# A third seven-product job, GLA factors in both directions at once, and transposes' banks freed by ScalarE

## The chip, the cores and the metric

One core of a Trainium2 chip runs one launch of the kernel. The metric is the device time of a launch in microseconds; times shown beside each other are of runs on the same chip. TensorE multiplies, VectorE, ScalarE and GpSimd (POOL) work element by element, and SyncE (SP) issues the DMAs in the order in which they are written.

## The reference

A layer of a hybrid backbone for 1024 latent tokens (width 1024) and 256 context tokens, in float32:

```python
p = modulate(rms_norm(x), sh, sc) @ w_in      # one projection, 9248 columns, also for the context
# columns: gq gk gv gg lr | dq dk dv dg | m_gla m_diff
# GLA: 4 heads, chunks of 64, both directions, decays from lr; the latent scans start from the context's state
scores = (q * exp(cum - ref)) @ (k * exp(ref - cum)).T ; o = tril(scores) @ v + (q * exp(cum)) @ state
state  = exp(last) * state + (k * exp(last - cum)).T @ v
# differential attention: 8 heads, queries 1024, keys 256 + 1024
a = softmax(s1) - lam * softmax(s2) ; o_diff = a @ v
y = sigmoid(m_gla) * (A @ w_br_gla) + sigmoid(m_diff) * (B @ w_br_diff)   # A, B: normed, SiLU-gated branches
out = x + g * (y @ w_out)
```

## The kernel before

The program is written by generators that run under a `Driver` (lines 57 to 185): a planner in plain Python that keeps a modelled time for each engine and resumes whichever generator is due, by priority. What it decides is only the order in which instructions stand in each engine's queue; on the chip they run in that order, each as soon as the semaphores allow. Its costs are in `Engine` (a fixed part and a part for each element) and `LAT` (the time until another engine sees a result). Every operation is issued through helpers, so the trace shows nearly all matmuls on L335, transposes on L361, all other engines' work on L197 and all DMAs on L300; tiles tell them apart.

Each matrix product in three matmuls (`mm3`): both operands are split into a high and a low part, by a copy of ScalarE and a subtraction of VectorE, and hi*hi, hi*lo and lo*hi are summed in PSUM. Tiles have a tag with a fixed number of buffers (`TAGS`); `acq` waits until one is free, `rel` gives it back. A buffer of PSUM (tags `mm`, `tp`, `gs`, `go`, `gt`, `mb`, `b1`, `mc`, ...) is one bank.

The stages, in order of time:

1. Normalisation, then jobs for gk, gq and half of gg, the decays (`job_la`), and sums of the normed input's quarters (`sums`), which go to DRAM.
2. `pairs` (L986): gv and then dv, each of 1024 columns, in seven products of half size (Winograd's form of Strassen's scheme) in place of eight. `pair_weights` (L917) makes the sums of weight quarters, 28 splits a job. Each product runs over 5 token tiles (4 latent, one of context), 4 k and 3 matmuls: 7 x 5 x 12 = 420 matmuls of 512 columns a job. TensorE's banks are `mm`, `gs`, `go` (A), `tp`, `gt` (B).
3. The late stage: `stream` runs dk0, gg1, dk1, dg0, dq0, MG0, dq1, dg1 (each 512 columns over 8 or 10 token tiles, 24 matmuls a tile). MG0 is the first half of the GLA branch's merge gate m_gla: 4 slices of 128 columns by 2 halves of the tokens, 8 half tiles of 24 matmuls; ScalarE takes the tanh and the result goes to `d_m`. Between them, with higher priority, stand the four GLA heads (`gla_head`, L1350). A head loads its keys and decays, sums the decays along each of 10 chunks of 128 and each direction (`prep`: 20 scans of 128 columns, with a `yield` after each), makes the state keys (`kstates`, tile `ge`), the inter-chunk queries (`gqe`) and for each pair of chunks and direction the factors `gqr` and `gkk` (in `intra`: subtractions of VectorE into `gd` and `gx`, exponents of ScalarE, products), then scores `gsc`, the states `gsb` and `gsf` and the output (`forward`, `post`, tile `gp`). Heads 1 and 3 lie in `hk`, the memory of the normed context, which is free (tag `hc`) when the second tile of dk1 has been projected. `job_gate` computes the residual gate's row `gb` on VectorE, from eight loads of `w_ada` into the tag `raw`, beside gg1.
4. When the stream has ended and GLA has (`to_gla`, `ev_b2`), the pools change and attention starts. `ev_b2` also lets the loads of queries (`aq`) and values (`vv`) go. 64 units (8 heads, 8 query tiles): scores for both softmaxes (`s`), maxima on VectorE, exponents `e` on ScalarE, the mix on VectorE, 10 transposes into banks of `b1` (`att_tr`), the split of the transposed weights (`split2`: of 10 blocks 8 by ScalarE's copy `ac` and GpSimd, the last 2 by ScalarE and VectorE from PSUM, tile `at`), products with the values (`att_av`) and for each two units the finish (`att_fin`, tile `b1k`) into `d_bT`.
5. Beside attention, at the lowest priority, `fill` (L1954) computes half tiles of 24 matmuls in the bank `mb`: the other 12 slices of the merge gates (kind 0), the 8 slices of A @ w_br_gla (kind 1), 40 half tiles that need no attention output, and then B @ w_br_diff (kind 2, 16 half tiles). The i-th may not start before unit `int(i * PACE)`. After the last scores the attention banks become `mc`, and the rest of the filler goes there; kind 2 needs `d_bT`.
6. The last projection, by seven products, with `gb` multiplied into w_out.

```python
            for c in (1, 0, 9, 8, 7, 6, 5, 4, 3, 2):                      # prep
                yield self.dve.tensor_tensor_scan(lab[:, c, 1:], self.ones, lab[:, c, 1:], 0.0, ALU.mult, ALU.add)
...
            e = self.act.activation(hi, pt, AF.Copy)                      # split2, pool is None
            yield On(e, "DVE")
            e = self.dve.tensor_tensor(lo, pt, hi.bitcast(F32), ALU.subtract)
            self.rel(tag, e)
```

## Time and profile before

| | |
|---|---|
| time, 3 runs | 1696.41, 1696.53, 1698.63 us |
| the profiled execution | 1694.84 us, span 1693.0 us, granted clock 0.995 |
| busy share of the span | PE 97%, weight loads 81%, DVE 70%, ACT 45%, POOL 36% |
| DMA | 292 MB, 173 GB/s on average |
| start of the seven-product jobs, late stage, attention | 208.26, 398.66, 912.35 us |
| last scores, start of the last projection's steady stretch | 1463.9, 1541.3 us |

A line of instructions has the line of the kernel, the engine, the operation, output<-input, the shapes and the count; behind the bar its busy time and the mean of one in ns; then the idle time just before it and what ended it. `128x512 f32` is 128 partitions of 512 columns.

### The profile page before, as it was taken

The page shows a single profiled execution, that of the slowest core. Times are in us where ns is not written, and L with a number is a line of the kernel's source. Part 1 is how long each engine was busy: PE and PEld are TensorE (multiplying, and loading weights), DVE is VectorE, ACT ScalarE, POOL GpSimd, SP SyncE. Part 2 cuts the span into 40 slices and gives each one's busy share as a digit, 9 for nine tenths or more (in the row PEclk, how much of TensorE's full clock was granted, in tenths as well). Part 3 has the DMA queues.
Part 4 walks back from the last instruction along what each step waited for, and adds up shares of the span by engine and source line. Part 5 has one row for each costly group of instructions (what it writes and reads, how often), then busy time and mean ns, then how long its engine had stood idle before and what let it go on. Part 6 is the DMA issues. An engine that isn't in the chain of part 4 may idle for free.

```text
span 1693.0 us, 24682 instructions
## 1 busy us (share of the span) xinstructions
PE 1647.7 (97%) x8437; PEld 1365.5 (81%) x8437; DVE 1179.3 (70%) x2179; ACT 766.4 (45%) x1564; POOL 603.4 (36%) x725
## 2 busy tenths in 40 slices
PE   8999999999999999999998999999999999999999
PEld 3788888888888888888886887888888778887887
DVE  4786853456877978875763888687777687735794
ACT  4666532243334245344342656556556455521231
POOL 1600200002554455543551554555545545620000
PEclk9999999999999999999999999999999999999999
DMA  8564847568457545644456244345267653269421
GB/s 304 169 217 177 329 158 271 182 245 304 131 171 246 165 144 157 189 149 138 125 152 180 72 131 128 116 124 141 80 172 240 177 155 101 75 197 360 159 100 75
DMA packets 255053, 292.38 MB, mean 173 GB/s; under 512 B 21928, under 2 KB 177488, under 8 KB 254928
## 3 DMA queue, kind: packets, MB, share of 16 engines
q1 hardware_dynamic: 254928, 290.80, 53.8%
q8 instruction: 67, 1.10, 0.3%
q14 instruction: 58, 0.48, 0.1%
HBM read 193.74 MB, written 96.99 MB: 172 GB/s over the span
## 4 chain that ended last, share of the span: by engine, by line
PE 87%; DMA 5%; DVE 3%; ACT 2%; POOL 1%; issue 1%; SPq 1%; ACTq 0%; DVEq 0%
PE mm L335 34%; PE mb L335 10%; PE mc L335 9%; PE s L335 8%; PE b L335 5%; PE go L335 4%; PE b L361 4%; PE tp L335 3%; PE gs L335 3%; PE gt L335 3%; PE tp L361 2%; DVE sm L197 1%; DMA w<-in_w_ada 1%; DMA h<-d_bT 1%; PE mz L335 1%
## 5 line engine op out<-in xcount | busy, mean ns | idle before, releaser
L335 PE MATMUL mm<-w,h 128*128 128x512 f32 x1608 | 405.9, 401 | 0.8 <-DVE w L197 0.8
L335 PEld LDWEIGHTS mm<-w,h 128*128 128x128 f32 x1608 | 296.8, 188 | 61.9 <-DVE w L197 2.0
L197 DVE TENSOR_REDUCE sm<-s 128x1 f32<-128x1024 f32 (+1 forms) x192 | 196.2, 1040 | 58.2 <-PE s L335 49.1
L335 PE MATMUL mb<-h,wt 128*128 128x512 f32 x816 | 221.1, 405 | 5.2 <-DVE ft L197 2.7
L335 PE MATMUL s<-hk,aq 128*128 128x512 f32 (+1 forms) x768 | 180.4, 368 | 11.0 <-ACT e L197 9.4
L197 POOL TENSOR_TENSOR at<-ac,at 128x512 fp32r<-128x512 f32 x128 | 187.0, 1461 | 10.7
L197 ACT ACTIVATE e<-s,sm 128x1280 f32<-128x1280 f32 x128 | 169.9, 1331 | 44.6 <-DVE sm L197 27.7
L197 POOL TENSOR_SCALAR at<-ac 128x512 fp32r<-128x512 f32 x128 | 95.1, 743 | 216.7 <-ACT ac L197 194.5
L335 PEld LDWEIGHTS mb<-h,wt 128*128 128x128 f32 x816 | 145.0, 190 | 32.3 <-DVE ft L197 4.0
L335 PEld LDWEIGHTS s<-hk,aq 128*128 128x128 f32 x768 | 123.0, 192 | 31.0 <-ACT e L197 13.7
L197 POOL TENSOR_SCALAR sm<-sm 128x1 f32<-128x1 f32 (+1 forms) x78 | 18.0, 231 | 360.9 <-DVE sm L197 262.9
L335 PE MATMUL mm<-h,w 128*128 128x512 f32 x576 | 145.4, 403 | 1.0 <-DVE h L197 1.0
L197 POOL TENSOR_TENSOR sm<-sm,nhalf 128x1 f32<-128x1 f32 (+2 forms) x110 | 112.9, 1026 | 64.0 <-DVE sm L197 57.4
L335 PE MATMUL b<-at,vv 128*128 128x256 f32 x960 | 129.8, 285 | 0.0
L335 PEld LDWEIGHTS mm<-h,w 128*128 128x128 f32 x576 | 108.0, 191 | 24.0 <-DVE h L197 1.8
L335 PEld LDWEIGHTS b<-at,vv 128*128 128x128 f32 x960 | 122.2, 190 | 3.9 <-ACT ac L197 0.3
L335 PE MATMUL mc<-h,wt 128*128 128x512 f32 x528 | 123.7, 392 | 1.1 <-DVE wt L197 0.5
L335 PEld LDWEIGHTS mc<-h,wt 128*128 128x128 f32 x528 | 98.1, 188 | 23.7 <-DMA h<-d_bT 2.1
L197 ACT ACTIVATE p<-mm 128x512 f32<-128x512 f32 (+1 forms) x111 | 63.9, 586 | 113.3 <-PE mm L335 95.4
L197 ACT ACTIVATE ac<-b 128x512 f32<-128x512 f32 x120 | 71.2, 601 | 95.4 <-PE b L361 92.8
L197 DVE TENSOR_TENSOR w<-raw,w 128x512 fp32r<-128x512 f32 x120 | 87.9, 749 | 32.3 <-ACT w L197 31.1
L197 DVE SCALAR_TENSOR_TENSOR e<-e,sm,e 128x1280 f32<-128x1280 f32 x64 | 104.4, 1631 | 0.8
(283 smaller groups left out, 2799.3 us busy)
## 6 DMA issues: line engine op xcount, KB each, us to landing
raw<-in_w_in SPq DMA_DIRECT2D x66, 512.0 KB, 4.4
g<-d_s SPq DMA_DIRECT2D x32, 640.0 KB, 5.2
aq<-d_qT SPq DMA_DIRECT2D x128, 128.0 KB, 3.0
d_dv<-pl SPq DMA_DIRECT2D x40, 256.0 KB, 2.3
d_kT<-pl SPq DMA_DIRECT2D x40, 256.0 KB, 2.6
gv<-d_v SPq DMA_DIRECT2D x40, 256.0 KB, 2.8
hk<-d_kT SPq DMA_DIRECT2D x32, 320.0 KB, 5.0
vv<-d_dv SPq DMA_DIRECT2D x16, 640.0 KB, 4.8
```

The lines of the kernel that those rows point to most:

```text
L197: self.ins = f(out, *args, **kw).ins
L335: self.ins = self.nc.tensor.matmul(out, lhsT, rhs, start=start, stop=stop, skip_group_check=more).ins
L361: self.nc.tensor.transpose(out, src, self.ident[:n, :n])
```

## The change

- `BY7` lists three jobs for `pairs`: gv, dv and now the first 1024 columns of the merge gates (m_gla). For the third the weights are the stationary operand and 512 tokens the moving one, there is no context tile, and the tanh of each result goes to `d_m`. MG0 leaves the stream, and `fill` starts at slice 8 (`fill_from`); `PACE` goes from 1.3 to 1.6.
- `job_gate` starts with the second seven-product job, uses a bank of `tp`, and stores `gb` to DRAM, from where it is loaded again ahead of the last projection. `to_gla` waits for it.
- A head's scans: three for each direction, over 2, 4 and 4 chunks, with a factor of 0 in the first column of each chunk.
- A reference value that was subtracted by VectorE ahead of an exponent is now ScalarE's bias, one chunk at a time (`ge` of the forward direction, `gqe` of the backward one, `gx`). The factors of the two directions are made by two generators at the same time; `gd` and `gx` have two buffers.
- `split2` without GpSimd and `att_fin`: ScalarE copies the bank to SBUF first, and what VectorE reads is that copy. `ac` 2 to 3, `b1k` 5 to 8, `fin` 2 to 3 buffers.
- The planner's fixed costs and `LAT` are other numbers.

```diff
-    LAT = dict(PE=0.24, ACT=0.15, DVE=0.15, POOL=0.15)
+    LAT = dict(PE=0.24, ACT=0.25, DVE=0.23, POOL=0.2)
...
-                c = 0.2 + 0.000833 * n + 0.093 * scalars - (0.028 if psum else 0.0) + (0.21 if acc else 0.0)
+                c = 0.095 + 0.000833 * n + 0.093 * scalars - (0.043 if psum else 0.0) + (0.091 if acc else 0.0)
...
-                c = 0.16 + 0.055 * scalars + n * 0.00104 * (
+                c = 0.07 + 0.055 * scalars + n * 0.00104 * (
...
-        for m in range(NM):
-            late.insert(5, tra(C_MG + m * 512, [0, 1], lambda s, half, pm, m=m: self.post_m(4 * m + s, half, pm)))
-        self.fill_from = 4 * NM
+        self.fill_from = 8
...
+    BY7 = (("gv", C_GV), ("dv", C_DV), ("mg", C_MG))
...
+            if what == "mg":
+                wt = [x[:, t * P:(t + 1) * P] for x in wp[g, W[n], k].w]
+                e = self.mm3(pm, *wt, *tokens(g, n, k), first, last, True)
+            else:
+                e = self.mm3(pm, *tokens(g, n, k, t), *wp[g, W[n], k].w, first, last, True)
...
+            nt = 4 if what == "mg" else 5
+            if g == 1:
+                d.spawn(self.job_gate(), prio=2)
...
+                if self.BY7[g][0] == "mg":
+                    self.act.activation(x, x, AF.Tanh, scale=0.5)
+                    self.store([(self.d_m[0][4 * c + t][:, r * 512:(r + 1) * 512], x)], (tag, 1))
+                    return
...
         yield self.ev_la
-        yield from self.idle("g5", "l5", "x4", "x2", "gs", "go", "gt")
+        yield self.ev_gb
+        yield from self.idle("gb", "g5", "l5", "x4", "x2", "gs", "go", "gt")
...
+        def sums(x):
+            for c, n in ((0, 2), (2, 4), (6, 4)):
+                y = x[:, c:c + n].rearrange("p c t -> p (c t)")
+                yield self.dve.tensor_tensor_scan(y, self.fresh[:, :n * (P + 1)], y, 0.0, ALU.mult, ALU.add)
...
-                    yield self.dve.tensor_tensor(ex, cf[:, sl, P - 1:P].to_broadcast([P, 2, P]), cf[:, sl],
-                                                 ALU.subtract)
-                yield self.act.activation(ex, arg, AF.Exp, scale=TAU)
+                    yield d.on("ACT", st["last"])
+                    for j in range(2):
+                        c = 2 * g + j
+                        en = self.act.activation(ex[:, j], st["cf"][:, c], AF.Exp, scale=-TAU, bias=st["last"][:, c:c + 1])
+                    yield en
...
+                    d.spawn(factors(e, g, qr, kr, ev[e]), prio=3)
+                for e in range(2):
+                    yield ev[e]
...
         yield from self.acq("ac")
         c = self.t("ac", [P, 4, P])[:, :pt.shape[1]]
         e = self.act.activation(c, pt, AF.Copy)
+        if pool is None:
+            e = self.act.activation(hi, pt, AF.Copy)
+            self.rel(tag, e)
+            yield On(e, "DVE")
+            e = self.dve.tensor_tensor(lo, c, hi.bitcast(F32), ALU.subtract)
+            self.rel("ac", e)
+            return e
...
+        yield from self.acq("b1k")
+        c = self.t("b1k", [P, 2, P])
+        self.rel("b1", self.act.activation(c, pt, AF.Copy))
         for x in range(2):
-            e = self.act.activation(oo[:, x], pt[:, x], AF.Square, accum_out=ss[:, x:x + 1])
+            e = self.act.activation(oo[:, x], c[:, x], AF.Square, accum_out=ss[:, x:x + 1])
```

`factors` is the body of the loop over the two directions that stood in `intra`, with one subtraction in place of two for `gd`, none for `gx`, and its exponents with a bias.

## Rows read from the trace of the kernel before

**Rows 1.** The page's busy table: engine, busy us, share of the span, instructions.
```profile
PE 1647.7 (97%) x8437; PEld 1365.5 (81%) x8437; DVE 1179.3 (70%) x2179; ACT 766.4 (45%) x1564; POOL 603.4 (36%) x725
```

**Rows 2.** Windows by stage: stretch, length, busy us (count) of each engine, clock, DMA.
```profile
208.26:398.66 190.40, 190.40 (x841) 157.71 (x841) 90.25 (x137) 64.06 (x111) 2.99 (x2) 1.00 0.63 225
398.66:912.35 513.69, 510.34 (x2516) 425.77 (x2516) 379.25 (x787) 200.36 (x509) 248.74 (x367) 1.00 0.55 168
912.35:1478.00 565.65, 539.48 (x3211) 461.14 (x3212) 434.25 (x828) 322.91 (x653) 293.69 (x275) 0.99 0.47 135
1478.00:1541.30 63.30, 62.17 (x318) 51.19 (x315) 17.66 (x40) 12.35 (x32) 14.67 (x16) 1.00 0.71 237
```

**Rows 3.** Groups of the late stage by form: VectorE's, and ScalarE's exponent of `gx`.
```profile
L197 DVE TENSOR_TENSOR_SCAN gla<-ones,gla 128x128 f32<-128x128 f32 x40 | 21.8, 568 | 0.0
L197 DVE TENSOR_TENSOR_SCAN hk<-ones,hk 128x128 f32<-128x128 f32 x40 | 18.7, 477 | 0.1
...
L197 DVE SCALAR_TENSOR_TENSOR gb<-raw,col,gb 128x512 f32<-128x512 f32 x14 | 11.0, 785 | 1.6 <-DMA raw<-in_w_ada 1.5
...
L197 ACT ACTIVATE gx<-gx 128x128 f32<-128x128 f32 x32 | 9.4, 294 | 0.0
...
L197 DVE TENSOR_TENSOR gx<-gla 128x128 f32<-128x128 f32 x16 | 6.0, 376 | 0.0
...
L197 DVE TENSOR_TENSOR gqe<-gla 128x256 f32<-128x256 f32 x8 | 4.6, 571 | 0.0
```

**Rows 4.** Timeline at the end of the late stage: start, us, engine, instruction, idle before.
```profile
902.31 0.38 PE L361 MATMUL tp<-ident,gp 128*128 128x128 f32 x2
902.45 8.45 PE L335 MATMUL mm<-w,h 128*128 128x512 f32 x36
...
910.16 5.44 SPq L300 DMA_DIRECT2D vv<-d_dv  x3
...
911.65 2.51 POOL L197 TENSOR_TENSOR p<-p,gdif 128x512 f32<-128x512 f32 x2 [9.16 <-DVE p L197]
...
915.70 2.55 SPq L300 DMA_DIRECT2D d_dg<-p  x2
...
922.72 1.33 ACT L197 ACTIVATE e<-s,sm 128x1280 f32<-128x1280 f32 x1 [11.19 <-DMA d_dg<-p]
...
924.20 2.08 PE L335 MATMUL s<-hk,aq 128*128 128x512 f32 x4 [5.19 <-ACT e L197]
```

**Rows 5.** Windows of ScalarE's exponents `gqr` alone: stretch, length, busy us (count).
```profile
540.00:611.00 71.00, 0.00 (x0) 1.00 0.66 200
611.00:912.00 301.00, 9.95 (x24) 1.00 0.49 148
```

**Rows 6.** A window just behind the pause of rows 4, columns as in rows 2.
```profile
923.00:929.00 6.00, 4.80 (x13) 4.03 (x14) 2.12 (x4) 2.45 (x4) 0.00 (x0) 0.50 0.02 5
```

**Rows 7.** TensorE's waits from 1000 to 1470: total us, times, longest.
```profile
PE b L361 <- DVE at L197: 4.3, 5, 1.9
PE b L361 <- DVE b1k L197: 4.0, 5, 2.0
PE s L335 <- ACT e L197: 2.9, 7, 1.0
```

**Rows 8.** Groups by form, attention's small splits; VectorE's `gqr` products, min/median/max in ns.
```profile
L197 DVE TENSOR_TENSOR at<-b,at 128x256 fp32r<-128x256 f32 x59 | 24.7, 418 | 17.0 <-ACT at L197 16.7
L197 ACT ACTIVATE at<-b 128x256 fp32r<-128x256 f32 x59 | 22.6, 383 | 23.5 <-PE b L361 23.3
...
L197 DVE TENSOR_TENSOR gqr<-gq,gqr x32: 405/420/1521, 465.3 to 882.1; 128x256 f32<-128x256 f32 x32
```

**Rows 9.** The page's group of the filler; windows of its matmuls after the last scores.
```profile
L335 PE MATMUL mb<-h,wt 128*128 128x512 f32 x816 | 221.1, 405 | 5.2 <-DVE ft L197 2.7
...
1463.87:1478.00 14.13, 6.42 (x24) 1.00 0.14 46
1478.00:1508.00 30.00, 19.79 (x80) 1.00 0.38 110
```

More of the change, by code (lines that the diff above doesn't have):

```diff
@@ L941, in run @@
             yield ev_run
-            for g in range(2):
+            for g in range(len(cols)):
                 def blk(n, k):
@@ L990, in loads @@
         def loads():
-            for g in range(2):
+            for g in range(len(self.BY7)):
                 for n in self.SUMS:
@@ L996, in loads @@
             yield self.ev_la
-            for g in range(2):
+            for g, (what, _) in enumerate(self.BY7):
+                w = 512 if what == "mg" else 640
                 for n in self.SUMS:
@@ L1081, in outer @@
                 return e
-            for t in range(5):
+            for t in range(nt):
                 yield from self.acq(TA[t])
@@ L1092, in pairs @@
                 for k in range(4):
-                    for t in range(5):
+                    for t in range(nt):
                         if k == 0:
@@ L1109, in pairs @@
             for k in range(4):
-                for t in range(5):
+                for t in range(nt):
                     if k == 0:
@@ L1119, in direct @@
         o = self.tok(8 if t == 4 else t)
-        if g == 0:
+        if self.BY7[g][0] == "mg":
+            yield from self.acq("p")
+            x = self.t("p", [P, 512])
+            self.rel(tag, self.act.activation(x, pm, AF.Tanh, scale=0.5))
+            self.store([(self.d_m[0][4 + t][:, :512], x)], ("p", 1))
+            return
+        if self.BY7[g][0] == "gv":
             yield from self.acq("p")
@@ L1480, in backward, with factors @@
                 self.rel("gv1", d.now)
+        def factors(e, g, qr, kr, ev):
+            sl = slice(2 * g, 2 * g + 2)
+            half = lambda x: x.rearrange("p c (s t) -> p c s t", t=64)
+            q4, k4 = half(st["q"][:, 2 * g - 2:2 * g]), half(st["k"][:, sl])
+            cc = half((st["cf"], st["eb"])[e][:, sl])
+            ref = cc[:, :, :, 31:32] if e == 0 else cc[:, :, :, 32:33]
+            yield from self.acq("gd")
+            yield from self.acq("gx")
+            yield from self.acq("gqr")
+            yield from self.acq("gkk")
+            dd = self.t("gd", [P, 2, 2, 64])
+            xd = self.t("gx", [P, 2, 64])
+            qq = qr[e] = self.t("gqr", [P, 2, 2, 64])
+            kk = kr[e] = self.t("gkk", [P, 2, 4, 64])
+            zb, xb = (1, 2) if e == 0 else (2, 1)
+            self.pool.memset(kk[:, :, zb], 0.0)
+            yield d.on("DVE")
+            self.dve.tensor_tensor(dd, cc, ref.to_broadcast([P, 2, 2, 64]), ALU.subtract)
+            sg = 1.0 if e == 0 else -1.0
+            yield self.d.when(dd)
+            self.act.activation(qq, dd, AF.Exp, scale=sg * TAU)
+            self.act.activation(dd, dd, AF.Exp, scale=-sg * TAU)
+            for j in range(2):
+                c = 2 * g + j
+                self.act.activation(xd[:, j], cc[:, j, e], AF.Exp, scale=-sg * TAU, bias=st[("rf", "rb")[e]][:, c:c + 1])
+            yield self.d.when(qq)
+            self.dve.tensor_tensor(qq, q4, qq, ALU.mult)
+            yield self.d.when(dd)
+            en = self.dve.tensor_tensor(kk[:, :, 0:4:3], k4, dd, ALU.mult)
+            self.rel("gd", en)
+            yield self.d.when(xd)
+            en = self.dve.tensor_tensor(kk[:, :, xb], k4[:, :, e], xd, ALU.mult)
+            self.rel("gx", en)
+            d.set(ev)
         def intra():
@@ L1866 @@
     PO, FI = "b1", "mb"
-    PACE = 1.3
+    PACE = 1.6
     PT, PA = 1, 2
```

161 lines of the change are left out of this document (65 added, 96 removed).

## The prediction

> **What bounds the kernel now.** I read the page's busy table first. TensorE is busy 97% of the span [rows 1], so time falls only where its work gets less or where one of its pauses goes. The stage table comes next [rows 2]; the reader is to see in each row how much of the stretch TensorE filled. The two seven-product jobs fill it wholly: 190.40 of 190.40 us for 841 matmuls, one of them of another job, so a matmul of 512 columns costs 190.4/840 = 0.2267 us. The late projections with the GLA heads woven in leave 3.4 us idle of 513.7. Attention with its filler leaves 26.2 us of 565.7, at 434 us of VectorE, which stands second. The stretch after the last scores leaves 1.1 us of 63.3. So the first question is how many matmuls go, the second where the attention stage's 26 us are, the third whether anything now hidden comes to light when TensorE's cover moves.
>
> **The change part by part.** The sum is made against the profiled execution, 1694.84 us (span 1693.0 plus 1.84 around it). The median shown, 1696.53, is 1.7 above it; that is added at the end.
>
> **1. The merge gate by seven products.** Removed are 16 half tiles of 24 matmuls, 384 in all: 192 of the stream job that stood between dq0 and dq1, and 192 of the filler (four slices of two halves). Added are seven products of 4 tiles, 4 k and 3 matmuls each, 336. The difference is 48 matmuls, 48 x 0.2267 = 10.9 us. The new job stands behind two of the same kind that never starve TensorE, but its 28 weight splits come in 336 matmuls (76.2 us) instead of 420 (95.2 us), so they must come 1.25 times as fast. VectorE was busy 90.25 of 190.40 us there and ScalarE 64.06 [rows 2], 47% and 34%; times 1.25 that is 59% and 42%. The gate job, moved beside the second and third products, adds 16 passes over 512 columns at about 0.785 us, 12.6 us of VectorE [rows 3], and 8 loads of the `raw` tag to SP's queue, whose transfers took 0.63 of the engines' time there. These stay hidden; if the cover were gone the 12.6 us of VectorE are the most that could show. GLA now waits for the gate too, but it waits for the third product's last sums anyway. Taken: -10.9, nothing for the rest, up to +5 in the range.
>
> **2. The late stage loses 192 matmuls, 43.5 us.** That comes off only if GLA ends early enough. Now it ends at 902.7, with the last transposes of `gp`, and the stream's last matmul ends at 910.9 [rows 4]. Unchanged, GLA would overhang a stream that ends at 910.9 - 43.5 = 867.4 by 35.3 us. What shortens it? For 71 us, from 540 to 611, no decay exponent of any head runs (0 of 32) [rows 5]: head 1 got its place in `hk` only when the second tile of dk1 was out, and then its 20 scans and head 2's stood one by one between the stream's VectorE work, each issued only after the one before had ended. Three long scans for each direction take their place. The scans are 40.5 us of VectorE in all [rows 3]; the elements stay, so I count on the turns, not on the busy time, and take half of the 71 us, 35. The other 24 exponents, two for each group of two chunks, take 301 us, 25 us a group; with both directions' factors in flight (`gd` and `gx` doubled) and the subtractions ahead of `ge`, `gqe` and `gx` gone (0.57 and 0.38 us for the last two and a hop to ScalarE each [rows 3]) I take 4 us off each of 12 groups, 48. Together 83, well over 35. ScalarE gains short exponents in their stead (0.29 us for 128 columns [rows 3], more with a bias), but it is busy 200 of 514 us. So GLA ends some 45 us ahead of the stream, and the 43.5 us come off; they are already inside the 10.9.
>
> **3. The passage to attention.** Now the GLA end and the stream end fall together, and that costs: the loads of `aq` and `vv` are issued only when GLA is through, and the last two stores `d_dg<-p`, ready when POOL ends at 914.16, leave SP at 915.70 behind `vv`, into full DMA engines. ScalarE's first exponent waits 11.19 us for them (the pool of `p` becomes the pool of `e`), and TensorE waits 5.19 us for that exponent [rows 4]. [...] If GLA is done early, those loads go out while the stream still computes, and the exponent can start some 5 us earlier. Bounds 0 and -7.6; taken -6, near the full row since one late store remains.
>
> **4. Banks freed by ScalarE alone.** In the attention stage TensorE's transposes wait 4.3 us for VectorE's `at` and 4.0 for its `b1k` [rows 7]; the first is the subtraction that holds a bank behind ScalarE's copy. Of the second, part is data (the scaled rows that are transposed next), which stays. Now a bank goes after ScalarE's one or two copies. The price is 128 more ScalarE copies of 256 columns (64 in the small transposes, 64 in the finish), 128 x 0.383 = 49 us [rows 8]: ScalarE goes from 323 to 372 of 566 us. It has room, but TensorE already waits 2.9 us for its exponents [rows 7], and that may double. Bounds -8.3 and +2.9; taken -4, half, for the doubt in the second row. [...]
>
> **5. Filler and tail.** The attention stage took 816/24 = 34 filler half tiles [rows 9] and left 6 of the 40 that need no attention output. Now there are 32, at most one per 1.6 units. Through the planner's new costs VectorE looks cheaper, so it will pack scores closer and put in fewer fillers. If all 32 went in, the stretch behind the last scores would lose its cover: in 1463.87 to 1508 fillers are 6.42 + 19.79 = 26.2 of 44 us [rows 9]. The first two output tiles can put 42 matmuls (9.5 us) of heads 0 to 6 in their place, and a shorter queue makes the chain itself shorter; I bound the loss by 13 us and 0, and take +3, since the cheaper VectorE leaves some filler over.
>
> **6. The new latencies and costs of the planner** reorder everything in the attention stage. What is left of its idle 26.2 us after parts 3 and 4 is some 10; so -10 on one side, and on the other a doubling of the whole, +26. Taken: 0.
>
> Sum: -10.9 - 6 - 4 + 3 = -17.9, so 1676.9 for an execution like the profiled one, and 1678.6 beside the median; I say 1679.
>
> **The rivals.**
> **A, the covers cancel:** the 10.9 us come off, but the fillers run out before the scores end and the passage stays as slow. 1696.5 - 10.9 - 4 + 13 = 1694.6; with the passage half gained 1691. For it: 34 half tiles fitted into the stage before, and only 32 are to be placed. Against: the planner's VectorE. Chance 0.2.
> **B, GLA becomes the bound (slower):** its chain is as long as before, and TensorE idles from 867 on. The late stage then gives back only 8 of its 43.5 us: 1696.5 - 10.9 - 4 + 35 = 1717. It decides from a GLA shorter by less than 35 us, and costs one for one below that; at a shortening of 15 us it is 1702. For it: the two end 8 us apart now. Against: the 71 us without an exponent. Chance 0.08.
> **C, denser attention stalls (slower):** with fillers moved behind it the stage has less of TensorE to hide VectorE's and ScalarE's latencies, and its 26 us of idle double: 1679 + 26 = 1705. It decides once the idle grows by 18 us. Ten fillers out, 10 x 24 x 0.2267 = 54 us, leave a stage of 511 us with 434 of VectorE, 85%, where it is 77% now [rows 2]. Chance 0.09.
> **D, the order is better than before:** parts 3 and 4 in full and the 10 us of part 6: 1696.5 - 10.9 - 7.6 - 8.3 - 10 = 1660. Chance 0.08.
>
> **How the numbers follow.** My forecast has 0.55, with a range of its own of 1668 to 1690. A measurement of this kernel tells 0.2% from no change, 3.4 us, so faster is below 1693.1 and slower above 1699.9. Faster: the forecast, D and under half of A, 0.72. Same: the rest of A and the mild ends of B and C, 0.12. Slower: 0.16. The range of 8 in 10 takes in A and the nearer part of D, and stops at the edge of B and C: 1663 to 1700.
>
> **What would show it.** Of the changed kernel's profile: a third stretch of gapless matmuls of some 76 us behind the first two; a late stage of some 470 us whose last `gp` transposes end tens of us before its last `mm`; `aq` and `vv` issued before the stream ends, no wait of the first exponent for `d_dg` over 6 us, and no row at clock 0.5 there; no wait of transposes for `at`, with ScalarE near 66% of the attention stage; filler half tiles left over after the last scores. I am wrong if `go` or `gp` work runs on behind the last `mm`, if TensorE's idle in the attention stage passes 40 us, or if it pauses for `d_bT` at the stage's end.

## The result, and the profile after

The changed kernel took 1702.15 us (median of 8 runs, 1699.54 to 1704.83) against 1695.67 us for the kernel before on the same chip (8 runs, 1693.68 to 1698.63): ratio 1.0042, 95% interval 1.0032 to 1.0052. It is slower by 0.4%; the forecast was 1679 and faster. Its profiled span is 1700.1 us, 7.1 above before.

The page's busy table of after answers to [rows 1]: TensorE's work has shrunk by 8 us only, and ScalarE has 67 us more.

```profile
PE 1639.8 (96%) x8389; PEld 1356.4 (80%) x8389; DVE 1204.2 (71%) x2071; ACT 833.4 (49%) x1788; POOL 614.2 (36%) x743
```

Windows of after by stage, columns as in [rows 2]: the first two seven-product jobs, the third one, the late stage, first to last scores, the 44 us behind them, and last, in one row, all from the first scores to the end.

```profile
207.50:397.90 190.40, 190.17 (x839) 157.00 (x838) 90.28 (x137) 62.35 (x108) 2.41 (x2) 1.00 0.66 231
397.90:474.00 76.10, 74.87 (x326) 60.62 (x325) 43.01 (x68) 31.07 (x55) 0.62 (x1) 1.00 0.73 248
474.00:943.98 469.98, 467.14 (x2333) 390.97 (x2331) 324.70 (x614) 207.90 (x562) 252.74 (x384) 1.00 0.58 170
943.98:1458.70 514.72, 475.62 (x2873) 404.33 (x2874) 453.41 (x805) 341.44 (x741) 289.64 (x266) 0.99 0.47 132
1458.70:1502.30 43.60, 43.60 (x269) 38.49 (x268) 23.37 (x50) 20.59 (x56) 24.55 (x24) 1.00 0.32 102
...
943.98:1700.10 756.12, 712.35 (x3984) 600.84 (x3984) 596.26 (x1034) 404.89 (x862) 314.19 (x290) 0.99 0.48 144
```

The same last stretch of the kernel before, in the same view:

```profile
912.35:1693.00 780.65, 749.52 (x4176) 634.20 (x4176) 562.37 (x1038) 374.21 (x746) 308.36 (x290) 0.99 0.48 146
```

The reader is to see two halves. Up to the first scores it went nearly as forecast: the third job leaves 1.2 of 76.1 us idle on TensorE, the late stage is 470 us, and the first scores come 31.63 us later than before (76.2 - 43.5 = 32.7 were forecast). In this the jobs start 2.4 us sooner (the first matmul into `tp` at 208.39 for 210.81), so counted from their start it is 34 us. From the first scores to the end 192 matmuls are gone, 43.5 us, and 7 us more were forecast; but the stretch is only 24.5 us shorter. TensorE's idle time there grew from 31.1 to 43.8 us, and 3984 matmuls cost 6 us more than 4176 less 43.5 would (749.5 - 43.5 = 706.0 against 712.4); 12.7 + 6.3 = 19.0 = 43.5 - 24.5. The 6 us aren't the clock's: summed over slices of 10 us, the granted clock falls short by 5.1 us in that stretch before and 5.8 after. They lie in the matmuls' records themselves (the filler's has a mean of 408 ns for 405 [rows 9], the scores' 372 for 368); why they are longer stays open.

TensorE's waits of after from 1000 to 1470, columns as in [rows 7]:

```profile
PE s L335 <- ACT e L197: 17.2, 25, 2.1
PE b L361 <- DVE b1k L197: 7.6, 6, 2.9
PE b L361 <- ACT ac L197: 2.9, 5, 1.0
```

The wait for VectorE's `at`, 4.3 us before, is gone as meant. In its place the scores wait 17.2 us for ScalarE's exponents, 2.9 before. ScalarE's own waits of after (945 to 1460), and then those of before:

```profile
ACT e L197 <- DVE sm L197: 92.9, 61, 5.3
ACT ac L197 <- PE b L361: 45.3, 53, 3.0
```

```profile
ACT ac L197 <- PE b L361: 87.0, 57, 5.8
...
ACT e L197 <- DVE sm L197: 27.7, 26, 3.0
```

Before, ScalarE mostly waited for TensorE's transposes. After, its exponents mostly wait for VectorE's maxima, and TensorE waits behind both: of the 20.6 us that it waits for exponents between first and last scores, 14.6 are for exponents ahead of which ScalarE itself had stood idle for a maximum. The page also follows the work that ended last back through whatever released it. In this chain, of before, of after and of e1 (the kernel after without the copies, below), VectorE's share of the span rises with the change, and ScalarE's does not:

```profile
PE 87%; DMA 5%; DVE 3%; ACT 2%; POOL 1%; issue 1%; SPq 1%; ACTq 0%; DVEq 0%
```

```profile
PE 70%; DVE 14%; DMA 6%; issue 4%; POOL 3%; ACT 2%; SPq 0%; ACTq 0%; DVEq 0%; POOLq 0%
```

```profile
PE 77%; DVE 8%; issue 4%; POOL 4%; DMA 3%; ACT 3%; SPq 1%; ACTq 0%; DVEq 0%; POOLq 0%
```

VectorE's groups by form in the attention stage answer to [rows 8]:

```profile
L197 DVE SCALAR_TENSOR_TENSOR e<-e,sm,e 128x1280 f32<-128x1280 f32 x63 | 113.2, 1797 | 0.4
L197 DVE TENSOR_TENSOR at<-ac,at 128x256 fp32r<-128x256 f32 x58 | 38.0, 655 | 2.3 <-ACT at L197 2.0
L197 DVE TENSOR_TENSOR b1k<-b1k,b1k 128x256 f32<-128x256 f32 x28 | 22.0, 785 | 0.3 <-ACT b1k L197 0.3
```

The subtraction that took 418 ns from PSUM takes 655 from the copy in SBUF. And the page's groups of the filler's half tiles, in the attention stage's bank `mb` and in `mc` behind it (before, x816 and x528), show what the planner made of it:

```profile
L335 PE MATMUL mc<-h,wt 128*128 128x512 f32 x600 | 140.1, 391 | 1.1 <-DVE wt L197 0.5
...
L335 PE MATMUL mb<-h,wt 128*128 128x512 f32 x552 | 154.5, 408 | 1.8 <-DVE ft L197 1.8
```

552/24 = 23 filler half tiles found a place in the attention stage's bank, not 34; the rest moved behind them, so the tail is covered (43.60 of 43.60 us) and the middle isn't.

### The profile page after: what moved, and what is told of

It is laid out like the page before. It is cut to its first block, busy times and chain, and to the rows that moved or that the text cites. A ratio compares the mean times of both kernels' runs of the same rounds, so it can differ in the third digit from the quotient of the medians.

```text
span 1700.1 us, 24862 instructions
## 1 busy us (share of the span) xinstructions
PE 1639.8 (96%) x8389; PEld 1356.4 (80%) x8389; DVE 1204.2 (71%) x2071; ACT 833.4 (49%) x1788; POOL 614.2 (36%) x743
## 4 chain that ended last, share of the span: by engine, by line
PE 70%; DVE 14%; DMA 6%; issue 4%; POOL 3%; ACT 2%; SPq 0%; ACTq 0%; DVEq 0%; POOLq 0%
PE mm L335 31%; PE mc L335 9%; DVE sm L197 7%; PE tp L335 5%; PE s L335 4%; PE go L335 4%; PE gt L335 3%; PE mb L335 3%; PE gs L335 3%; DVE e L197 3%; PE b L335 3%; PE b L361 2%; PE tp L361 2%; DVE b1k L197 2%; POOL at L197 2%
## 5 line engine op out<-in xcount | busy, mean ns | idle before, releaser
L335 PE MATMUL s<-hk,aq 128*128 128x512 f32 (+1 forms) x768 | 185.5, 372 | 22.7 <-ACT e L197 20.6
L197 DVE TENSOR_REDUCE sm<-s 128x1 f32<-128x1024 f32 (+1 forms) x192 | 194.5, 1036 | 10.2 <-PE s L335 7.9
L197 POOL TENSOR_SCALAR at<-ac 128x512 fp32r<-128x512 f32 x128 | 106.3, 831 | 207.5 <-ACT ac L197 197.5
L335 PE MATMUL mb<-h,wt 128*128 128x512 f32 x552 | 154.5, 408 | 1.8 <-DVE ft L197 1.8
L335 PE MATMUL mc<-h,wt 128*128 128x512 f32 x600 | 140.1, 391 | 1.1 <-DVE wt L197 0.5
L197 ACT ACTIVATE ac<-b 128x512 f32<-128x512 f32 (+1 forms) x213 | 105.0, 506 | 61.7 <-PE b L361 55.8
L335 PEld LDWEIGHTS mc<-h,wt 128*128 128x128 f32 x600 | 111.5, 188 | 25.6 <-DMA h<-d_bT 1.6
L197 POOL TENSOR_TENSOR sm<-sm,nhalf 128x1 f32<-128x1 f32 (+2 forms) x110 | 113.5, 1032 | 29.2 <-DVE sm L197 22.7
L197 DVE SCALAR_TENSOR_TENSOR e<-e,sm,e 128x1280 f32<-128x1280 f32 x64 | 115.8, 1809 | 0.4
L335 PEld LDWEIGHTS mb<-h,wt 128*128 128x128 f32 x552 | 97.4, 191 | 17.9 <-DVE ft L197 2.3
L197 ACT ACTIVATE w<-raw 128x512 fp32r<-128x512 f32 x128 | 77.2, 626 | 69.0 <-DVE raw L197 21.6
L335 PE MATMUL mm<-h,w 128*128 128x512 f32 x420 | 99.6, 392 | 2.0 <-DVE h L197 1.1
L361 PE MATMUL b<-ident,e 128*128 128x128 f32 x604 | 90.0, 274 | 4.1 <-ACT ac L197 2.9
```

The lines of the kernel that those rows point to most:

```text
L197: self.ins = f(out, *args, **kw).ins
L335: self.ins = self.nc.tensor.matmul(out, lhsT, rhs, start=start, stop=stop, skip_group_check=more).ins
L361: self.nc.tensor.transpose(out, src, self.ident[:n, :n])
```

## The experiments

From the first scores to the end every kernel with the third job has 3984 matmuls, every one without it 4176, so that stretch can be compared between kernels; "the stretch" below is this one, taken from each profile. Its values with TensorE's idle time:

| kernel | time, us | first scores | the stretch | idle in it | half tiles of filler in `mb` |
|---|---|---|---|---|---|
| before | 1694.6 to 1696.5 | 912.4 | 780.6 (less 43.5: 737.1) | 31.1 | 34 |
| after | 1702.15 | 944.0 | 756.1 | 43.8 | 23 |
| no copies (e1) | 1690.93 | 945.1 | 743.4 | 35.2 | 32 |
| planner's old costs (e2) | 1719.73 | 960.9 | 756.2 | 44.5 | 22 |
| no copies, old costs (e3) | 1717.78 | 960.2 | 755.2 | 40.2 | 32 |
| before + copies (e4) | 1720.40 | 913.9 | 804.4 (760.9) | 48.8 | 22 |
| copies, VectorE from PSUM (e5) | 1711.54 | 945.1 | 764.9 | 50.4 | 32 |
| copies, bank held (e6) | 1712.06 | 944.5 | 761.7 | 48.3 | 32 |
| no copies, pace 2.3 (e7) | 1711.56 | 944.8 | 762.0 | 45.9 | 29 |
| before + new costs (e8) | 1690.65 | 915.8 | 774.9 (731.4) | 24.6 | 31 |
| spare copies (e9) | 1704.97 | 945.0 | 756.7 | 44.3 | 32 |
| finish's 32 copies alone (e10) | 1692.77 | 945.0 | 745.5 | 34.6 | 27 |
| splits' 96 copies alone (e11) | 1703.36 | 946.0 | 754.9 | 38.1 | 26 |

The time of before is the range of its medians beside these runs; the ratios given below are to before on the same chip.

**e1: VectorE's reads and the bank's release as before.** The kernel after with `split2` and `att_fin` of before.

```diff
+        if pool is None:
+            e = self.act.activation(hi, pt, AF.Copy)
+            yield On(e, "DVE")
+            e = self.dve.tensor_tensor(lo, pt, hi.bitcast(F32), ALU.subtract)
+            self.rel(tag, e)
+            return e
         yield from self.acq("ac")
         c = self.t("ac", [P, 4, P])[:, :pt.shape[1]]
         e = self.act.activation(c, pt, AF.Copy)
-        if pool is None:
...
-        self.rel("b1", self.act.activation(c, pt, AF.Copy))
...
+        self.rel("b1", max(e, e2))
```

> The changed kernel with the small split and the finish as before, VectorE reading PSUM and the 128 extra copies of ScalarE gone. Theory P (operands): moved from PSUM to SBUF, VectorE's two-operand instructions run into GpSimd's accesses: at 418 to 655 ns, the finish's two 418 and 415 to 785 and 633 ns, about 30 us of VectorE in a stage where it is 88% busy. P expects them back at 0.42 us and 15 to 25 us less: 1677 to 1687. Theory O (order): the planner's cheaper VectorE packs the scores closer and moves 11 filler half tiles behind the stage, and TensorE has too little to do while it waits. O expects 1697 to 1704, and TensorE still idle for 35 us or more of the attention stage.

1690.93 us, ratio to before 0.9977 (0.9968 to 0.9986). Windows of e1, the stretch, its attention stage and the 80 us behind it:

```profile
945.12:1688.50 743.38, 708.21 (x3984) 598.07 (x3984) 560.89 (x1034) 367.03 (x734) 306.31 (x290) 0.99 0.49 147
945.12:1482.50 537.38, 515.99 (x3082) 439.07 (x3083) 430.03 (x817) 312.17 (x631) 281.32 (x266) 1.00 0.50 145
1482.50:1522.50 40.00, 35.56 (x224) 30.13 (x224) 20.24 (x48) 16.04 (x41) 24.98 (x25) 1.00 0.61 195
1522.50:1562.50 40.00, 34.25 (x142) 27.84 (x141) 25.36 (x39) 6.34 (x8) 0.00 (x0) 0.91 0.72 243
```

The copies and what comes with them cost 12.7 us of the stretch. 21.4 us idle in the attention stage is less than before's 25.6, but all 32 fillers went in, and the tail lost its cover: 10.2 us idle in 80 and a clock of 0.91. In that tail TensorE waits once for the first output tiles' data:

```profile
PE mc L335 <- DMA h<-d_bT: 5.8, 1, 5.8
```

**e2 and e3: the planner's old latencies and costs,** in the kernel after and in e1. (The fixed costs go back too.)

```diff
-    LAT = dict(PE=0.24, ACT=0.25, DVE=0.23, POOL=0.2)
+    LAT = dict(PE=0.24, ACT=0.15, DVE=0.15, POOL=0.15)
...
-                c = 0.07 + 0.055 * scalars + n * 0.00104 * (
+                c = 0.16 + 0.055 * scalars + n * 0.00104 * (
```

> The changed kernel with the planner's latencies and costs of before, all else as changed. O expects 30 or more filler half tiles back beside the scores, TensorE idle some 26 us there and 1680 to 1690, with a loss of up to 13 us behind the last scores where no filler is left. P expects VectorE's SBUF operands as slow as in the changed kernel (at near 0.6 us) and 1695 to 1705.

> The changed kernel with both undone: split and finish from PSUM, and the planner's old costs; the merge gate's seven products, the GLA factors and PACE 1.6 stay. P alone: as without the SBUF operands, 1677 to 1687. O alone: as with the old costs, 1680 to 1690. If both count, below either by 5 us or more. By the matmul count and the attention stage of before 1696 - 11 = 1685, and up to 13 us more where the filler runs out.

1719.73 (ratio 1.0148, 1.0134 to 1.0162) and 1717.78 (1.0139, 1.0123 to 1.0154). The old costs put the first scores 17 us later; 13.4 of it is in the jobs and the late stage, whose window in e2 is the first row (after: 735.6 us for the same 3489 matmuls), the stretch the second:

```profile
211.93:960.89 748.96, 734.75 (x3489) 609.08 (x3488) 451.61 (x816) 302.72 (x725) 266.16 (x387) 1.00 0.59 189
960.89:1717.10 756.21, 711.67 (x3984) 599.17 (x3984) 609.07 (x1036) 401.55 (x863) 309.65 (x289) 1.00 0.49 147
```

So the new costs don't lose the time; with the new GLA code they are worth 17.6 us. With the old ones the copies make only 1.0 us of difference to the stretch, since e3's is 12 us longer than e1's too: this pair doesn't show the loss.

**e4: the banks' part alone in the kernel before** (`split2`, `att_fin` and three buffer counts of after).

```diff
-ac=("sbB", 2), b1k=("sbB", 5), fin=(None, 2)
+ac=("sbB", 3), b1k=("sbB", 8), fin=(None, 3)
...
+            self.rel(tag, e)
-            e = self.dve.tensor_tensor(lo, pt, hi.bitcast(F32), ALU.subtract)
+            e = self.dve.tensor_tensor(lo, c, hi.bitcast(F32), ALU.subtract)
```

> The kernel before with only the split and the finish through ScalarE's copies (and their buffers), planner's costs as before. P: VectorE gets some 30 us more to do in the attention stage, which is 77% busy there: 1700 to 1715. O, and the prediction's fourth part: banks come free earlier, 1688 to 1697, and VectorE's operations stay at 0.42 us.

1720.40, ratio 1.0154 (1.014 to 1.0168). The stretch is 23.8 us longer than before, with 22 fillers for 34: more than the 19.0 us by which the whole change falls short, from one part.

**e5 and e6: which ingredient?** e5 keeps ScalarE's copies but lets VectorE read PSUM, with the bank held for it; e6 keeps VectorE on the copies but holds the bank until VectorE is done.

```diff
             e = self.act.activation(hi, pt, AF.Copy)                            # e5
+            yield On(e, "DVE")
+            self.rel("ac", e)
+            e = self.dve.tensor_tensor(lo, pt, hi.bitcast(F32), ALU.subtract)
             self.rel(tag, e)
-            yield On(e, "DVE")
-            e = self.dve.tensor_tensor(lo, c, hi.bitcast(F32), ALU.subtract)
...
-            self.rel(tag, e)                                                    # e6
             yield On(e, "DVE")
             e = self.dve.tensor_tensor(lo, c, hi.bitcast(F32), ALU.subtract)
+            self.rel(tag, e)
```

> The kernel after, with ScalarE's 128 added copies left in and used by ScalarE's squares, but VectorE's subtractions and products read the bank in PSUM again and the bank is held until VectorE is done. It splits the first run (both operands back, copies gone: 1690.9 against 1702.1) into its two ingredients. Theory O (operands): VectorE's instructions with two SBUF operands are stretched by GpSimd's traffic (at<-ac 655 ns, b1k<-ac 633, e 1797 in mean); reading PSUM they go back to 415 to 418 ns and the exponential's product to about 1.65 us: VectorE's busy time of the attention stage 425 to 435 us, its idle TensorE 20 to 28, and 1688 to 1694 us in all. Theory S (ScalarE's 49 us of copies are what the stage lacks): VectorE's durations go back but the time stays at 1699 to 1704, with TensorE's waits on ScalarE's e unchanged at 15. Theory R (the packing that earlier banks make): also 1688 to 1694, but then the next run comes out there too.

> The kernel after with its SBUF operands for VectorE, but the bank is given back only when VectorE is done, as in the kernel before: the planner loses the earlier banks and nothing else changes. Theory O: the stretched instructions stay (at<-ac 640 to 700 ns, VectorE 445 to 460 us busy in the stage), so 1698 to 1712. Theory R (the order that the earlier banks let the planner make is what costs): the time falls to 1688 to 1694 although VectorE's instructions stay long. If the earlier bank is worth what the forecast took for it (4 us of TensorE's wait), this run is 2 to 6 us slower than the kernel after.

1711.54 (1.0098, 1.0084 to 1.0111) and 1712.06 (1.0094, 1.0082 to 1.0107). The windows from first to last scores, e5 first, show VectorE back at 432 us in the one and at 455 in the other, and TensorE idle 34 us in both:

```profile
945.09:1499.40 554.31, 519.97 (x3068) 439.56 (x3069) 431.94 (x815) 345.02 (x740) 291.30 (x264) 0.99 0.49 141
```

```profile
944.48:1497.20 552.72, 518.57 (x3068) 438.62 (x3069) 454.74 (x816) 345.31 (x740) 296.78 (x264) 1.00 0.50 142
```

My theory at that point, that VectorE's stretched instructions are what costs, fell for kernels that hold the bank: e5 has none of the three stretched forms (0.414 to 0.417 us in mean there) and is no faster than e6 in the stretch. What both share, and e1 has not, is ScalarE's copies, and with them a bank that is held for one copy longer; this pair can't tell the two apart, e9 does. Holding the bank costs 5.6 us (e6 against after), so the earlier bank is worth something, about what the forecast took for it. Whether VectorE's stretch costs where the bank goes early, as in after, no run tells: VectorE can't read a bank that has been given back.

**e7: fewer fillers between the scores,** e1 with another pace.

```diff
-    PACE = 1.6
+    PACE = 2.3
```

> The first run's kernel (VectorE reads PSUM) with the fillers' pace at 2.3 units a half tile instead of 1.6. There 32 half tiles lay inside the attention stage and the 80 us behind it had 10 us of idle TensorE at a clock that fell to 0.91. At 2.3 no more than 28 can lie inside (63 units by 2.3). If the fillers that are missing behind the scores are the cause of that loss, four half tiles (22 us) move behind the last scores, the stage is 19 to 24 us shorter, the tail's TensorE is busy 39 of 40 us again, and the whole is 1679 to 1688. If the attention stage can't do without them (TensorE waits for VectorE there whatever fills it), the stage shortens by 10 us or less and the whole is 1690 to 1700.

1711.56, 1.0096 (1.0082 to 1.011): slower than either branch. Holding three half tiles back shortened the stage by nothing (538.2 against 537.4 us), idle rose there from 21 to 35, and the 40 us from 1523 were still at 34.5 us busy and clock 0.91. In this order the attention stage needs its fillers. The change's own step, 1.3 to 1.6, does nothing: the programs with either are the same, instruction for instruction, in after and in e1.

**e8: the new costs alone in the kernel before.** (The fixed costs change too.)

```diff
-    LAT = dict(PE=0.24, ACT=0.15, DVE=0.15, POOL=0.15)
+    LAT = dict(PE=0.24, ACT=0.25, DVE=0.23, POOL=0.2)
...
-                c = 0.16 + 0.055 * scalars + n * 0.00104 * (
+                c = 0.07 + 0.055 * scalars + n * 0.00104 * (
```

> The kernel before with the planner's new cost model and latencies and nothing else. The kernel after lost 17.6 us when it was given the old ones back. If that gain belongs to the cost model as such (it fits the chip's durations better, whatever the kernel), this kernel is faster than before by 5 to 15 us: 1680 to 1690. If it belongs to the new GLA code, which the old costs mistime (the late stage then ended with GLA at 955.7 instead of with the stream at 942.5), this kernel stays within 4 us: 1691 to 1699. The forecast's own bound was -10 to +26.

1690.65, 0.9972 (0.9963 to 0.9982). The late stage is 3.5 us longer, the stretch 5.7 us shorter.

**e9: ScalarE's time alone.** e1 with 128 copies of tiles that ScalarE has just written, into buffers that nothing reads.

```diff
+            self.rel("ac", self.act.activation(c, hi.bitcast(F32), AF.Copy))     # split2, behind the release
...
+        self.rel("b1k", self.act.activation(c, oo, AF.Copy))                     # att_fin
```

> The first run's kernel (VectorE reads PSUM, 1690.9) with ScalarE's 128 extra copies added again, but as spare work: each copies a tile in SBUF that ScalarE has written just before, into a buffer that nothing reads, and no bank waits for it. Theory S (ScalarE's time: some 30 us more busy in the attention stage, in front of the exponentials): about 1711, as with the copies on the path; TensorE's idle in the stage 33 to 36 us. Theory L (the latency that the copy puts between transpose and split, not its time): 1689 to 1695, idle 20 to 24.

1704.97, 1.0045 (1.0033 to 1.0058). The stretch is 13.4 us longer than e1's though nothing reads a copy. (The copies still take turns in the buffers of `ac` and `b1k`, and the planner plans with their time.) Windows of e9, from first to last scores and the 47 us behind:

```profile
944.96:1488.60 543.64, 518.21 (x3086) 440.26 (x3087) 427.50 (x816) 347.73 (x739) 288.64 (x264) 1.00 0.52 150
1488.60:1536.10 47.50, 37.12 (x221) 32.70 (x220) 16.74 (x49) 21.66 (x61) 24.92 (x27) 0.86 0.31 88
```

Here 6.3 us of the loss lie between first and last scores and 7.1 behind them (10 us idle in 47.5, at a granted clock of 0.86). In after all of it lies between the scores: the stage is 22.7 us shorter than e1's where nine half tiles less, 9 x 24 x 0.2267, are 49, so 26 are lost there, and 14 are won behind. The same loss has two forms.

**e10 and e11: the two halves of the copies.** e10 has `split2` of before (the finish's 32 copies stay), e11 has `att_fin` of before (the splits' 96 stay).

```diff
-            e = self.dve.tensor_tensor(lo, c, hi.bitcast(F32), ALU.subtract)     # e10
+            e = self.dve.tensor_tensor(lo, pt, hi.bitcast(F32), ALU.subtract)
...
-        self.rel("b1", self.act.activation(c, pt, AF.Copy))                      # e11
```

> The kernel after with the splits as before (ScalarE rounds the bank, VectorE subtracts from PSUM; 96 copies gone) and the finish still by ScalarE's copy (32 stay). If each copy costs alike, three quarters of the 11 us between 1702.1 and 1690.9 come back: about 1694. If the finish is the guilty one (its copy stands in front of the two squares): about 1700 or more.

> The kernel after with the finish as before (squares and VectorE's product from PSUM; 32 copies gone) and the splits still by ScalarE's copies (96 stay). If each copy costs alike: about 1699. If the finish alone is guilty: about 1691. Together with the other half this also shows whether the two halves add up to the 11 us.

1692.77 (0.998, 0.9969 to 0.999) and 1703.36 (1.0038, 1.0025 to 1.005). In the stretch the 32 copies of the finish cost 2.2 us over e1 and the 96 of the splits 11.6, some 0.1 us a copy; together 13.8 beside the 12.7 of both. But e11's whole time is above after's 1702.15, where 1699 was expected if each copy costs alike. TensorE's waits of e11 (945 to 1475) name the engine:

```profile
PE s L335 <- ACT e L197: 11.1, 15, 2.2
PE b L361 <- DVE b1k L197: 7.2, 8, 2.1
PE b L361 <- ACT ac L197: 7.1, 8, 1.5
PE b L361 <- ACT at L197: 2.1, 3, 0.8
```

Between first and last scores TensorE's waits that ScalarE ended sum to 8.8 us in e1 (13.0 in before), 16.0 in e10, 21.1 in e11 and 24.4 in after. In e9 they are 15.1. They do not follow the loss: e10 has 16.0 and loses 2.2 us, and the spare copies under another order (order_s22 below) have 11.1 beside 10.1 of the same order without copies, and lose 13.0.

**Orders.** The planner lays out everything again for every edit, so how much is the order alone worth? These runs change one modelled latency by a hundredth or two (GpSimd's 0.20 to 0.19, 0.21, 0.22; in before 0.15 to 0.16) and no instruction.

```diff
-    LAT = dict(PE=0.24, ACT=0.25, DVE=0.23, POOL=0.2)
+    LAT = dict(PE=0.24, ACT=0.25, DVE=0.23, POOL=0.21)
```

> The first run's kernel with the planner's latency for GpSimd at 0.21 instead of 0.20: not one instruction more or less, only another order, from the product stage on. It sizes what the planner's order alone is worth. If orders of equal merit differ by 3 us or less (1688 to 1694), the differences of 9 to 21 us between the runs before stand for what was edited. If this alone moves the time by 8 us or more, differences of that size between single kernels of this study can't be put down to the edit.

> The kernel after with the planner's latency for GpSimd at 0.21 instead of 0.20; only the order differs. From the first scores to the end the kernel after took 756.1 us and the one with the banks as before 743.4 and 744.0. If the loss is the edit's: 752 to 765 here. If it was the order's: anywhere from 738 to 765, also below 748.

> As the run before with 0.22: 752 to 765 us from the first scores to the end if the loss is the edit's, below 748 possible if it is the order's.

> The kernel with the banks as before (VectorE reads PSUM, no copies) with 0.19: 740 to 748 us from the first scores to the end if the edit is what costs, above 752 possible if it is the order.

> The kernel with the banks as before (no copies) with 0.22: 740 to 748 us from the first scores to the end if the copies are what costs, above 752 possible if it is the order.

> The spare copies again (128 ScalarE copies that nothing reads and no bank waits for, VectorE from PSUM) with the planner's latency for GpSimd at 0.22; its twin without copies took 743.3 us from the first scores to the end. If ScalarE's time is what costs: 750 to 760. If the first pair's 13 us were its order: 740 to 747.

> The kernel before with the planner's latency for GpSimd at 0.16 instead of 0.15; only the order differs. If 1694.6 is a typical time for its instructions, this one lies within 5 us of it; if it is the best of many orders, this one is 6 to 20 us slower, and the same part of the loss of the kernel after is the order's.

| latency | after | no copies (e1) | spare copies (e9) |
|---|---|---|---|
| 0.19 | | 1693.64; stretch 745.7 | |
| 0.20 | 1702.15; 756.1 | 1690.93; 743.4 | 1704.97; 756.7 |
| 0.21 | 1711.62; 753.9 | 1703.99; 744.0 | |
| 0.22 | 1707.52; 752.2 | 1702.68; 743.3 | 1715.96; 756.3 |

The order alone moves the whole time by up to 13 us, but nearly all of that ahead of the first scores: at 0.21 and 0.22 the jobs start 8 us later and the late stage takes 5 us more, with copies or without. The windows of the stretch at 0.21 (no copies, first fence; after, second) and of spare copies at 0.22 (third):

```profile
958.18:1702.20 744.02, 710.88 (x3984) 600.80 (x3984) 554.50 (x1034) 366.38 (x734) 310.28 (x290) 0.99 0.48 144
```

```profile
956.66:1710.60 753.94, 712.30 (x3984) 600.82 (x3984) 596.40 (x1034) 404.95 (x862) 314.26 (x290) 0.99 0.47 143
```

```profile
959.84:1716.10 756.26, 716.23 (x3984) 605.32 (x3984) 554.17 (x1034) 408.17 (x862) 315.84 (x290) 0.98 0.48 142
```

In the stretch the groups don't touch: 743.3 to 745.7 without copies in four orders, 752.2 to 756.7 with them in five, order by order 12.7, 9.9 and 8.9 us for after and 13.4 and 13.0 for the spare copies. Of the last pair's 13.0, 7.0 us are TensorE's busy time, at a granted clock of 0.98 for 0.99; this is its window without copies:

```profile
959.03:1702.30 743.27, 709.18 (x3984) 599.72 (x3984) 554.61 (x1034) 366.43 (x734) 310.73 (x290) 0.99 0.48 145
```

The kernel before at 0.16 took 1700.77 us, ratio 1.0031 (1.0019 to 1.0042), its stretch 785.3, 4.7 us longer than at 0.15, while e8's is 5.7 shorter: its own order is neither the best nor a bad one. Orders of one kernel spread the stretch by 2.4 to 4.7 us, so e10's 2.2 us and the 3.2 between e5 and e6 are not clear of the order, and e6's 5.6 hardly is.

## Why the prediction was wrong

The forecast summed to -17.9 us for the profiled execution, and 7.1 were measured, a miss of 25.0: 1.1 better than forecast up to the first scores (with 2.4 from the jobs' earlier start), 26.0 worse behind them.

**Part 4 is the step that failed.** It took -4 us, with bounds of -8.3 and +2.9, for banks that go "after ScalarE's one or two copies", and said of the 49 us of copies that ScalarE "has room". The edit costs 12.7 us in this order and 9 to 13 in three, a miss of 16.7. The gain was read rightly from [rows 7] (the wait for `at` is gone, and the earlier bank is worth about 5.6 by e6), but the price was booked as next to nothing because ScalarE was busy 57% of the stage, 66% with the copies. The runs show in its place that 128 copies cost the stretch 9 to 13 us, some 0.1 us or a quarter of its 0.383 for each, whether their result is used or not (e9, order_s22). Three pairs of runs show that the edit costs it, and two that the copies' time on ScalarE, without the rest of the edit, costs as much. The exception is the pair under the old costs, 1.0 us (e2, e3); in before the edit came with 23.8 (e4).

How a copy's time reaches TensorE stays open, and the nearest guess, an exponent late because it stands behind a copy in ScalarE's queue, is not what the trace of after shows: there most of TensorE's waits for exponents lead back to VectorE's maxima. One rival is untested: in after, part of the 12.7 us can be VectorE's longer instructions, which e5 takes away only together with the early bank. That e9 comes to the same number by another form may then be chance.

The other 9.3 us of the miss are in e1 too (its stretch is 6.3 us above before's less 43.5, where parts 3 and 5 had forecast 3 below): parts 5 and 3, next, make 5.2 and 3.0 of it.

Part 4 also gave no price to VectorE's reads from SBUF. [rows 8] held a sign of one: VectorE's `gqr` products, from SBUF, have a median of 420 ns beside 418 for the subtraction from PSUM, but a maximum of 1521. Reading the copies stretched VectorE by 58 x 0.24 + 28 x 0.37 + 28 x 0.22 = 30 us in the attention stage. That was a real loss of VectorE, to 453 of 515 us; with the bank held, giving it back gains nothing (e5 against e6).

**Part 5** took +3 for fillers and tail. In e1, where part 4 is undone, TensorE's idle time behind the last scores is 13.8 us for 5.6 before, 8.2 us lost: rival A's mechanism, below its price of 13. In after the same shortage took the other form, 23 fillers between the scores and a covered tail. The reason that the part gave for fewer fillers, the planner's cheaper VectorE, isn't borne out: the kernel after has 22 with the old costs and 23 with the new, e1 32 with either.

**Rival C** is how the changed kernel lost, in its own numbers: ten fillers out, a stage of 511 us with VectorE at 85%, idle up and 1705 us were foretold at a chance of 0.09; eleven out, 514.7 us, 88%, idle of 39.1 for 25.6, and 1702.15 came. Its cause was not fewer fillers in themselves: e10 has 27 and loses little. Nor do the copies make that packing. It goes with the bank that is given back early: 22 to 27 half tiles in after, e2, e4, e10 and e11, 32 in e5, e6 and e9, which have copies and hold the bank.

**Parts 1 and 2 were right.** Three jobs almost without a gap, 31.63 us later at the first scores instead of 32.7. GLA starts late, since it waits for the gate, and not for the third product as I had said. Timeline of after, SP's store of the gate and the first load of a head; the third job had ended at 476:

```profile
499.92 0.33 SPq L300 DMA_DIRECT2D d_gb<-gb  x1
501.84 0.69 SPq L300 DMA_DIRECT2D gk<-d_k  x1
```

It still ends ahead of the stream, at 927.5 against 942.5: 418 us from the first scan to the last transposes instead of 489, a shortening of 71 where 83 were taken and, with the later start, about 56 were needed. ScalarE's exponents with a bias took 0.39 us for 128 columns (`ge` and `gqe` of after), where `gx` without one had taken 0.29 [rows 3]. TensorE at the end of the late stage, after:

```profile
927.13 0.38 PE L361 MATMUL tp<-ident,gp 128*128 128x128 f32 x2
927.26 15.26 PE L335 MATMUL mm<-w,h 128*128 128x512 f32 x66
943.98 1.27 PE L335 MATMUL s<-hk,aq 128*128 128x512 f32 x5 [1.46 <-issue]
```

Rival B stayed away only with the new costs: with the old ones (e2) GLA began 21 us later, ended at 955.7, 2.7 us ahead of the stream, and TensorE idled 14 of the 749 us up to there.

**Part 3** took -6. `d_dg` still leaves behind `vv`, but TensorE's pause went from 5.19 to 2.19 us and the granted clock there from 0.50 to 1.00. The timeline of after answers to [rows 4], the window to [rows 6]:

```profile
945.22 2.43 SPq L300 DMA_DIRECT2D d_dg<-p  x2
...
951.34 1.33 ACT L197 ACTIVATE e<-s,sm 128x1280 f32<-128x1280 f32 x1 [8.19 <-DMA b1k<-d_dg]
...
952.81 1.20 PE L335 MATMUL s<-hk,aq 128*128 128x512 f32 x4 [2.19 <-ACT e L197]
```

```profile
948.00:954.00 6.00, 3.81 (x17) 2.86 (x16) 0.38 (x3) 2.66 (x4) 0.00 (x0) 1.00 0.56 175
```

The first exponent stands 7.36 us behind the first scores instead of 10.37: 3.0 us came. ScalarE's wait of 8.19 us for that load is above the 6 that the forecast had named as its limit. Of the 7.6 us that bounded the term, 5.19 are TensorE's wait [rows 4]; the other 2.4, for the clock, no run shows. What the runs show in their place: at a granted clock of 0.50 four matmuls of `s` took 2.08 us [rows 4] and the three of the filler behind them 1.49, at 1.00 in after the same took 1.20 and 0.85. By these seven, 3.57 us for 2.05, the 4.80 us of TensorE's work in [rows 6] held some 2.0 to be won, my estimate. The 0.50 is gone from this place, but over the whole stretch the granted clock falls short by 5.8 us in after for 5.1 before: it is 0.83 from 989 to 999, from 1118 to 1128 and from 1337 to 1347.

**Part 6** took 0 for the new costs, bounded by 10 us gained, and looked at the attention stage alone. They are worth 4.6 us in the kernel before (e8) and 17.6 in after, there nearly all ahead of the first scores (the stretch is 756.2 with the old costs, 756.1 with the new); without the copies they shorten the stretch too, by 11.8 us (e1 against e3).

One size was missing altogether: how much of either kernel's time is its order. The kernel before stands in a middling order (e8 and order_b16 lie 4.6 us below it and 4.3 above), and any edit that makes the planner lay out the instructions anew draws again. Without the copies the change is worth what e1 and its orders show, 1690.9 to 1704.0 us, around the kernel before; e1 and e8, 1690.93 and 1690.65, beat both kernels, each by 4 us over before.

## What to carry to other kernels

Copies that freed a bank sooner were not free here, though ScalarE was busy only 57% of the stage: 128 of them cost the stretch 9 to 13 us, some 0.1 us of the 0.383 of each. Price such copies, and put in spare copies that nobody reads to measure that price by itself. A wait names the engine that ended it; ask of that engine, too, what it had waited for. Where a planner re-orders everything after an edit, change one irrelevant number to see what the order alone is worth before crediting the edit, and compare stretches that hold the same instructions rather than whole times. Read the maximum of a row beside its median: here, 1521 ns beside 420 from SBUF before, it was the maximum that gave warning of the 633 to 785 ns in mean that VectorE's reads of the copies took after.

## What the runs showed of the hardware

VectorE's instructions with two operands in SBUF often took longer where one of GpSimd's with two operands overlapped them. In after, 51 of the 256-column `at`, `b1k<-b1k,b1k` and `b1k<-ac` instructions from the first scores on ran with no two-operand instruction of GpSimd at work, and none took over 0.43 us; the 77 that met one took 0.77, 1.04 and 0.89 us in mean, between 0.41 and 1.52. Two lines of VectorE and then GpSimd's of after's timeline:

```profile
1160.98 0.43 DVE L197 TENSOR_TENSOR at<-ac,at 128x256 fp32r<-128x256 f32 x1
...
1161.46 1.39 DVE L197 TENSOR_TENSOR b1k<-b1k,b1k 128x256 f32<-128x256 f32 x1
```

```profile
1160.52 0.62 POOL L197 TENSOR_SCALAR at<-ac 128x512 fp32r<-128x512 f32 x1 [3.50 <-ACT ac L197]
1161.22 1.33 POOL L197 TENSOR_TENSOR at<-ac,at 128x512 fp32r<-128x512 f32 x1
```

VectorE's second instruction ends at 1162.85, 0.30 us behind GpSimd's end at 1162.55; the first, which began 0.24 us ahead of GpSimd's two-operand instruction, took 0.43. With GpSimd's passes of one operand both occur: such a pass ran from 1091.95 to 1092.69, and VectorE's `at` that began at 1092.12 took 0.83 us and ended 0.26 us behind it, while the 14 that met such a pass alone took 0.41 to 0.42. From PSUM the same work took 415 to 418 ns in mean (e1, before); the 47 of before that met a two-operand instruction of GpSimd took 416 in mean and none over 0.43 us. The 37 of after that met nothing of GpSimd's took 407 to 427 ns from SBUF, about what they took from PSUM.
